# Writing out every engine's queue order in a fused decoder step, in place of pins, priorities and a chain

## The chip, the cores and the metric

The kernel runs on one core of a Trainium2 chip. The core has TensorE (PE in the profile, its weight loads PEld), VectorE (DVE), ScalarE (ACT), GpSimd (POOL) and SyncE (SP), each with a queue of its own that it works off in order; an instruction at the head of a queue waits by semaphores for what other engines and transfers have to deliver, and what stands behind it on that engine waits with it. The metric is device time in microseconds (us) of one execution, the median over runs.

## The reference

One layer of a decoder with two token mixers, run on a prompt of 512 tokens and on 8 sample tokens that have 1024 cached positions each; D_MODEL is 1024, heads are 64 wide.

```python
shift, scale, gate = jnp.split(jax.nn.silu(c) @ w_ada + b_ada, 3, axis=-1)
h = x * (1.0 + scale[:, None, :]) + shift[:, None, :]
parts = jnp.split(h @ w_in, np.cumsum(IN_WIDTHS)[:-1], axis=-1)
(a_q, a_kc, a_vc, a_ks, a_vs, a_kw, a_vw, a_g, a_z, b_q, b_k, b_v, b_z, m_a, m_b) = parts
...
ck = compress(cmp_seq[:, :, 0], phi_pos[0], phi_w1[0], phi_b1[0], phi_w2[0], phi_b2[0])   # gelu(blk @ w1 + b1) @ w2 + b2
cv = compress(cmp_seq[:, :, 1], phi_pos[1], phi_w1[1], phi_b1[1], phi_w2[1], phi_b2[1])
...
o_a = nsa_attention(...)     # gates[0] * compressed + gates[1] * selected blocks + gates[2] * window
o_b = moba_attention(...)    # top blocks by q . mean(k), and the own block
y_a = (o_a.reshape(bsz, t, NSA_WIDTH) * jax.nn.silu(a_z)) @ w_up_a
y_b = (o_b.reshape(bsz, t, MOBA_WIDTH) * jax.nn.silu(b_z)) @ w_up_b
mixed = (jax.nn.sigmoid(m_a) * y_a + jax.nn.sigmoid(m_b) * y_b) @ w_out
x_new = layer_norm(DEEPNORM_ALPHA * x + gate[:, None, :] * mixed, ln_g, ln_b)
```

The new rows of each cache are outputs as well.

## The kernel before

Everything runs in fp32 on TensorE's fp32r path, where each product is made of three matmuls: both operands are split into a high part (a cast, mostly on ACT: weights `hl` at L305, cache rows `u` at L877) and the rest (`lo`, a subtraction on DVE or POOL, L226). A dense product `d` thus takes `hTh` with both parts of the weights and `hTl` with the high part, all through `mm` (L172); transposes go through `tr` (L191).

The stages, by the time of the profile: the adaLN vectors and the modulated input (0 to 42 us); the compression network "phi" over the prompt and over four pairs of cache pages (42 to 145), in which a page is loaded into `craw`, split into `u`, multiplied with the first weight matrix (`s<-u,w1h`), put through a gelu (`t1`, then `gl`, split like the rest), and multiplied with the second (`pt<-gl,w2h`); the sample tokens' compressed branch (145 to 181); attention of eight head pairs for the prompt, with the sample tokens' decode over cache pages between them (181 to 507); the last of that decode (to 536); the up and output projections (536 to 626); the norms (to 647). Dense products ("fills", lists of column blocks of w_in and others) are interleaved with all stages but the last by `merge`, which takes the next step of the flow that is furthest behind its planned time.

Loads are issued by SP through `ld` (L199) and by POOL for gathers. The weights come through a feed of 4 raw buffers and 3 split ones, decode pages (`raw<-slck`, `raw<-mobk`, `raw<-mobv`) through a ring of their own, so a load's issue waits until its buffer was last read.

The order of each engine's queue is settled by a scheduler that simulates the program, bound by what the code pins. `order` adds a dependency without a semaphore, used for `in_turn` (while `behind[0]` is set, TensorE's instructions stay in the order of the trace) and for the chain of loads in `ld` (once `queue[0]` is set). `issue_after` keeps an instruction behind another one's issue, `high_priority` lifts it in the scheduler. `together` keeps the matmuls of a group adjacent, and can make the first of them wait, with a semaphore, for instructions given to it: in `value` these are three copies of transposed probabilities.

In the attention the scores `s` of a head come through `probs` (DVE adds the bias and takes the maximum at L1096, ACT exponentiates at L1099, DVE takes the reciprocal at L1100, POOL or DVE scales at L1101), are transposed to `pt`, copied to `pp` (L1110) and multiplied with the values to `o`.

## Time and profile before

| | |
|---|---|
| median of 3 runs | 648.98 us (646.98 to 650.88) |
| profiled execution, own time | 648.92 us |
| its span, first to last instruction | 647.1 us |
| mean granted TensorE clock | 0.976 |
| TensorE busy | 604.3 us (93%) |
| weight loads, DVE, ACT, POOL busy | 509.2, 320.7, 296.4, 289.5 us |
| DMA | 124.80 MB, mean 193 GB/s |

The busy times are added over the whole span, so they hide which stage waits for what; the waits and the stretches shown with the prediction tell that. A matmul's "mean ns" is its latency, and matmuls overlap, so the number of matmuls times that is more than the busy time. The granted clock is the share of full speed at which TensorE was allowed to run.

### The profile page before, as it was taken

To read this page: it belongs to the slowest core of one execution; us is meant where nothing else is said; L and a number is where in the kernel's file an instruction comes from. 1 tells how busy PE (TensorE), PEld (TensorE's weight loads), DVE (VectorE), ACT (ScalarE), POOL (GpSimd) and SP (SyncE) were. 2 spreads that over 40 slices of the span, in tenths; PEclk is the share of its full clock that TensorE was granted. 3 is DMA by queue.
4 is the path that set the end of the run, shared out by engine and by line. 5 is a ranking of instruction groups with operands and counts; after the bars stand their busy time and mean duration, and the time that the engine had idled before them with its cause. 6 is when DMAs were issued, how large, how long until landed. Compare 5 with 4: busy or idle time off the path is not lost.

```text
span 647.1 us, 13273 instructions
## 1 busy us (share of the span) xinstructions
PE 604.3 (93%) x4709; PEld 509.2 (79%) x4709; DVE 320.7 (50%) x818; ACT 296.4 (46%) x680; POOL 289.5 (45%) x328
## 2 busy tenths in 40 slices
PE   5999899979999999999998999989999989999993
PEld 2789799979988868867767898977766669799672
DVE  3467365342476558545454454684432125545277
ACT  3367355423446537645444455555442232433621
POOL 2033665442463623532435634363332326465646
PEclk9999899969999999999999999999999989999997
DMA  8985645422345495268895754712878966344302
GB/s 313 406 286 185 195 148 158 144 73 66 98 128 168 146 332 192 75 224 273 277 349 172 236 185 156 226 49 71 276 264 304 403 231 214 132 165 141 120 31 102
DMA packets 63956, 124.80 MB, mean 193 GB/s; under 512 B 8402, under 2 KB 26642, under 8 KB 63378
## 3 DMA queue, kind: packets, MB, share of 16 engines
q1 hardware_dynamic: 62482, 119.76, 55.0%
q0 software_dynamic: 1408, 4.20, 1.9%
q8 instruction: 37, 0.61, 0.4%
q14 instruction: 29, 0.24, 0.1%
HBM read 114.34 MB, written 9.58 MB: 191 GB/s over the span
## 4 chain that ended last, share of the span: by engine, by line
PE 58%; DMA 7%; DVE 7%; issue 5%; SPq 4%; ACT 4%; POOL 2%; POOLq 0%; ACTq 0%; DVEq 0%
PE d L172 33%; PE s L172 8%; PE e L172 6%; SPq L199 4%; PE pt L191 3%; PE o L175 2%; PE o L172 2%; DMA craw<-cmp 2%; DMA raw<-w_cols 2%; DMA xw<-bw 1%; PE pt L172 1%; PE e L175 1%; DMA raw<-slcv,vidx 1%; DMA raw<-mobk 1%; DVE u L226 1%
## 5 line engine op out<-in xcount | busy, mean ns | idle before, releaser
L172 PE MATMUL d<-hTh,hl 128*128 128x260 f32 (+1 forms) x1408 | 273.7, 291 | 1.5 <-DVE hl L226 1.0
L172 PEld LDWEIGHTS d<-hTh,hl 128*128 128x128 f32 (+1 forms) x1408 | 218.7, 188 | 25.3 <-issue 18.5
L172 PE MATMUL d<-hTl,hl 128*128 128x260 f32 (+1 forms) x704 | 199.6, 283 | 0.0
L172 PEld LDWEIGHTS d<-hTl,hl 128*128 128x128 f32 (+1 forms) x704 | 131.9, 187 | 0.3
L226 POOL TENSOR_TENSOR hl<-raw,hl 128x512 fp32r<-128x512 f32 x57 | 74.9, 1314 | 89.0 <-ACT hl L305 85.6
L305 ACT CAST hl<-raw 128x512 fp32r<-128x512 f32 (+1 forms) x111 | 67.9, 616 | 73.1 <-PE d L172 62.2
L1099 ACT ACTIVATE p<-s,sm 128x512 f32<-128x512 f32 (+1 forms) x96 | 50.6, 528 | 69.5 <-DVE sm L1096 57.1
L1101 POOL TENSOR_SCALAR p<-p,sm,gp 128x512 f32<-128x512 f32 (+1 forms) x64 | 42.7, 669 | 75.1 <-DVE sm L1100 73.5
L226 DVE TENSOR_TENSOR hl<-raw,hl 128x512 fp32r<-128x512 f32 (+1 forms) x54 | 51.5, 953 | 48.0 <-ACT hl L305 47.3
L172 PE MATMUL d<-yh,hl 128*128 128x260 f32 x256 | 46.6, 284 | 0.0
L191 PE MATMUL pt<-cst,p 128*128 128x128 f32 x240 | 39.3, 279 | 2.5 <-POOL p L1101 1.8
L172 PEld LDWEIGHTS d<-yh,hl 128*128 128x128 f32 x256 | 39.6, 188 | 2.4 <-ACT yh L1485 0.8
L1096 DVE CUSTOM_DVE_ANT_0 s<-s,band 128x256 f32<-128x256 f32 (+1 forms) x48 | 17.4, 363 | 47.5 <-PE s L172 42.2
L1101 POOL TENSOR_SCALAR p<-p,sm,cst 128x512 f32<-128x512 f32 (+3 forms) x32 | 20.4, 640 | 39.7 <-DVE sm L1100 39.5
L172 PE MATMUL s<-u,w1h 128*128 128x256 f32 (+1 forms) x160 | 33.7, 307 | 3.1 <-POOL u L226 3.1
L172 PE MATMUL d<-yl,hl 128*128 128x260 f32 x128 | 35.8, 284 | 0.4 <-DVE yl L226 0.4
L172 PE MATMUL s<-kd,q 128*128 128x512 f32 (+1 forms) x96 | 33.3, 346 | 1.3 <-ACT p L1099 1.3
L191 PEld LDWEIGHTS pt<-cst,p 128*128 128x128 f32 x240 | 27.7, 142 | 7.6 <-POOL p L1101 4.7
L226 POOL TENSOR_TENSOR u<-craw,u 128x512 fp32r<-128x512 f32 x16 | 22.6, 1419 | 21.1 <-ACT u L877 20.1
L172 PEld LDWEIGHTS s<-u,w1h 128*128 128x128 f32 x160 | 28.7, 217 | 3.3 <-POOL u L226 3.3
L172 PE MATMUL s<-kd,qx 128*128 128x512 f32 (+1 forms) x96 | 30.9, 322 | 0.0
L172 PEld LDWEIGHTS s<-kd,q 128*128 128x128 f32 x96 | 18.2, 189 | 15.2 <-issue 8.3
(417 smaller groups left out, 1141.7 us busy)
## 6 DMA issues: line engine op xcount, KB each, us to landing
raw<-w_cols SPq DMA_DIRECT2D x46, 512.0 KB, 5.0
raw<-mobk SPq DMA_DIRECT2D x64, 256.0 KB, 4.1
raw<-mobv SPq DMA_DIRECT2D x64, 256.0 KB, 4.9
craw<-cmp SPq DMA_DIRECT2D x64, 128.0 KB, 2.2
u<-ada_ss SPq DMA_DIRECT2D x12, 512.0 KB, 9.0
raw<-slck SPq DMA_DIRECT2D x64, 64.0 KB, 2.1
raw<-ada_g SPq DMA_DIRECT2D x8, 512.0 KB, 4.7
raw<-w_up SPq DMA_DIRECT2D x8, 512.0 KB, 4.8
```

Source lines behind the costliest of these rows:

```text
L172: i = mmraw(out, lhsT, rhs, start=start, stop=stop, skip_group_check=True)
L175: i = mmraw(out, lhsT, rhs, start=start, stop=stop, skip_group_check=True)
L191: return in_turn(nc.tensor.transpose(out, x, unit))
L199: i = nc.sync.dma_start(out, x)
L226: (nc.gpsimd if eng == "p" else nc.vector).tensor_sub(out, x, f32(hi))
L305: nc.scalar.copy(h, src)
L1096: nc.vector.tensor_tensor_reduce(out=s[:, b:n], in0=s[:, b:n], in1=j.band[:, 256 - (n - b):], scale=1.0, scalar=top, op0=OP.add, op1=OP.mi ...
L1099: nc.scalar.activation(pr, s[:, :n], AF.Exp, scale=-1.0, bias=sm[:, 1:2], accum_out=sm[:, 2:3])
L1101: D.setdefault("pool", []).append(nc.gpsimd.tensor_scalar(pr, pr, sm[:, 3:4], j.gate(i), op0=OP.mult, op1=OP.mult))
```

## The change

A table `QUEUES` lists, for each of the five engines, runs of indices into that engine's instructions in the order in which the program makes them, and `line_up`, called once after the kernel is built, turns each list into a chain of dependencies without semaphores. What pinned the order before is taken out: `order`, `in_turn`, `together` (with its semaphore waits on the three copies), `issue_after` and `high_priority` at all their places, and the chain of loads. `behind` becomes `steady`, a mere flag, and `queue[0]` becomes `D['late']`, which still sets how far ahead weights are loaded.

```diff
+QUEUES = {
+    "PE": """
+0-471 521-526 473-496 472 497-520 527-886 932-937 896-919 887-895 920-931 938-1275 1288-1289 1276-1287 1290-1363 1368-1371 1364-1367 1372-1379
...
+}
...
+def line_up(tc):
+
+    traced = tc.nc.cur_bb.bb.instructions
+    for name, text in QUEUES.items():
+        mine = [i for i in traced if i.engine == getattr(mybir.EngineType, name) and i.opcode != "TilePoolBoundary"]
+        queue = []
+        for run in text.split():
+            a, _, b = run.partition("-")
+            queue += mine[int(a):int(b or a) + 1]
+        assert len(queue) == len(mine) == len({i.name for i in queue})
+        for before, i in zip(queue, queue[1:]):
+            tc.add_manual_dep(i, before.name, mybir.DependencyInfo(mybir.DependencyClass.NoSync, mybir.DependencyReason.DATA),
+                              reason="queue")
...
-    glue, behind, queue = [False, None], [False, None], [False, None]
+    steady = [False]
 
     def mm(out, lhsT, rhs, start, stop):
-        if glue[1] is None:
-            i = mmraw(out, lhsT, rhs, start=start, stop=stop, skip_group_check=True)
...
-        return in_turn(i)
+        return mmraw(out, lhsT, rhs, start=start, stop=stop, skip_group_check=True)
...
     def ld(out, x):
-
-        i = nc.sync.dma_start(out, x)
-        if queue[0]:
-            if queue[1] is not None:
-                order(i, queue[1])
-            queue[1] = i
-        return i
+        return nc.sync.dma_start(out, x)
...
-            with tc.high_priority():
-                return gelu(us, n)
+            return gelu(us, n)
...
-            with together([js[1].copied[k] for k in range(3)]):
-                for kb in range(4):
...
+            for kb in range(4):
```

Against the queues of before, 75 of TensorE's 4209 instructions move, 15 of 578 on ACT, 19 of 722 on DVE, 8 of 330 on POOL and 3 of 514 on SP; the others keep their order. Most moves stand at 0 to 13, 73 to 85, 129 to 145, 181 to 245, 327 to 390, 429 to 447, 478 to 509 and 519 to 530 us of the profile. Three of the places follow; in the changed kernel line numbers are higher (L172 becomes L244, L175 is its sibling form, L191 becomes L247, L226 becomes L260, L641 becomes L667).

POOL at 69 to 78 us, in the first compression stage: `u_794` is the small part of a cache page, `gd` the sample tokens' gates, which eight small transfers rearrange, `hl_994` and `hl_1130` weights of the dense fills. Before:

```order
L226 TENSOR_TENSOR u_795<-craw_842,u_795 128x4x16x8
L641 DMA gd_82<-gs_922 8x1x3 x8
L226 TENSOR_TENSOR hl_994<-raw_819,hl_994 128x512
L226 TENSOR_TENSOR u_794<-craw_885,u_794 128x4x16x8
L226 TENSOR_TENSOR hl_1130<-raw_819,hl_1130 128x512
L226 TENSOR_TENSOR u_1091<-craw_958,u_1091 128x4x16x8
```

Now:

```order
L260 TENSOR_TENSOR u_795<-craw_842,u_795 128x4x16x8
L667 DMA gd_82<-gs_922 8x1x3 x2
L260 TENSOR_TENSOR u_794<-craw_885,u_794 128x4x16x8
L667 DMA gd_82<-gs_922 8x1x3 x2
L260 TENSOR_TENSOR hl_994<-raw_819,hl_994 128x512
L667 DMA gd_82<-gs_922 8x1x3 x4
L260 TENSOR_TENSOR hl_1130<-raw_819,hl_1130 128x512
L260 TENSOR_TENSOR u_1091<-craw_958,u_1091 128x4x16x8
```

The second split of `u_794` (from `craw_885`) stands behind two of the eight transfers in place of all eight and a weight split.

TensorE at 129 us, at the end of the compression stage: `pt_1778` is the second product of a page pair's network, which reads the gelu `gl_1616`; `s_1791` is the first product of the next pair's; `d_1831` and `d_1699` are dense fills. Before:

```order
L172 MATMUL d_1699<-hTl_74,hl_1702 128x260
L172 MATMUL pt_1778<-gl_1616,w2h_113 128x256
L172 MATMUL pt_1778<-gl_1616,w2l_114 128x256
L172 MATMUL pt_1778<-gl_1616,w2h_113 128x256
L172 MATMUL pt_1778<-w2h_113,gl_1616 128x64
L172 MATMUL pt_1778<-w2l_114,gl_1616 128x64
L172 MATMUL pt_1778<-w2h_113,gl_1616 128x64 x2
L172 MATMUL pt_1778<-w2l_114,gl_1616 128x64
L172 MATMUL pt_1778<-w2h_113,gl_1616 128x64
L172 MATMUL s_1791<-u_1619,w1h_111 128x256
L172 MATMUL s_1791<-u_1619,w1l_112 128x256
L172 MATMUL s_1791<-u_1619,w1h_111 128x256 x2
```

Now:

```order
L244 MATMUL d_1699<-hTl_74,hl_1702 128x260
L244 MATMUL d_1831<-hTh_73,hl_1751 128x260 x2
L244 MATMUL d_1831<-hTl_74,hl_1751 128x260
L244 MATMUL d_1831<-hTh_73,hl_1751 128x260 x2
L244 MATMUL d_1831<-hTl_74,hl_1751 128x260
L244 MATMUL s_1791<-u_1619,w1h_111 128x256
L244 MATMUL s_1791<-u_1619,w1l_112 128x256
```

Six dense matmuls of `d_1831` and all 24 of `s_1791` stand ahead of `pt_1778`, which follows behind the last of `s_1791`. On POOL the split of `gl_1616` goes ahead of one of `u_1620` at the same place.

TensorE at 520 us: `e_6597` is the product of the last mobv cache page with the sample tokens' probabilities `tp_5955`; `d_7080` is an up projection, `d_6962` and `d_6963` are dense fills. Before:

```order
L172 MATMUL d_7080<-yh0_6744,hl_6966 128x260 x2
L172 MATMUL d_7080<-yl0_6745,hl_6966 128x260
L172 MATMUL e_6597<-raw_6903,tp_5955 32x512
L175 MATMUL e_6597<-raw_6903,tp_5955 32x512 x3
L172 MATMUL d_6963<-hTh_73,hl_6884 128x260 x2
L172 MATMUL d_6963<-hTl_74,hl_6884 128x260
```

Now:

```order
L244 MATMUL d_6962<-hTh_73,hl_6929 128x260 x2
L244 MATMUL d_6962<-hTl_74,hl_6929 128x260
L244 MATMUL e_6597<-raw_6903,tp_5955 32x512 x4
L244 MATMUL d_6963<-hTh_73,hl_6929 128x260 x2
L244 MATMUL d_6963<-hTl_74,hl_6929 128x260
```

`e_6597` stands behind 18 dense matmuls (the second half of a block of `d_6963` and twelve of `d_6962`) that it preceded.

Around 431 us, on ACT the exponential of a score block (`p_5871`) goes ahead of an evacuation, a weight cast and a copy to `pp`; on DVE a weight split (`hl_5911`) goes behind two reciprocals and the scaling `xm`; on TensorE the four transposes `pt_5942` go 18 matmuls later.

## The prediction

> **What bounds the kernel now.** I read the page first, for the busy shares and the clock row, then the view of what the engines wait for, cut to TensorE, then a table of stretches around the longest of those waits, and last the timeline at four places.

> ```profile
> span 647.1 us, 13273 instructions
> PE 604.3 (93%) x4709; PEld 509.2 (79%) x4709; DVE 320.7 (50%) x818; ACT 296.4 (46%) x680; POOL 289.5 (45%) x328
> ```

> TensorE is busy 604.3 of 647.1 us; no other engine passes half. So the time is TensorE's work, its idle time, and the time in which it works at half clock. The second is this list (engine, line, what it waited for: us in total, times, longest):

> ```profile
> PE s L172 <- DMA u<-ada_ss: 7.5, 4, 5.1
> PE s L172 <- POOL u L226: 3.1, 1, 3.1
> PE e L172 <- DMA raw<-mobv: 3.0, 1, 3.0
> PE pt L172 <- ACT gl L817: 2.9, 1, 2.9
> PE pt L191 <- ACT pp L1110: 1.9, 4, 0.8
> PE e L172 <- DMA raw<-slcv,vidx: 1.9, 1, 1.9
> PE pt L191 <- POOL p L1101: 1.8, 1, 1.8
> PE pt L172 <- POOL gl L226: 1.5, 1, 1.5
> PE s L172 <- ACT p L1099: 1.3, 2, 1.1
> PE pt L172 <- DVE gl L226: 1.1, 1, 1.1
> PE d L172 <- DVE hl L226: 1.0, 1, 1.0
> PE d L191 <- DVE v L607: 0.8, 1, 0.8
> PE d L191 <- ACT ev L576: 0.6, 1, 0.6
> PE d L172 <- ACT hl L305: 0.5, 1, 0.5
> ```

> These rows sum to 28.9 us, and seven shorter ones of the view, none above 0.5, add some 2: waits of single instructions at the head of TensorE's queue, behind which everything else on it stands. The half clock is in the stretches (start:end, length, then busy time of PE, its weight loads, DVE, ACT and POOL, the granted clock, DMA share, GB/s):

> ```profile
> 76.60:80.20 3.60, 3.59 (x18) 3.59 (x19) 0.00 (x0) 0.00 (x0) 1.19 (x1) 0.55 0.67 172
> 129.27:134.44 5.17, 0.80 (x2) 0.50 (x2) 4.43 (x5) 3.33 (x8) 5.09 (x5) 0.73 0.68 205
> 134.44:141.00 6.56, 6.55 (x30) 6.56 (x31) 2.11 (x5) 0.72 (x2) 1.18 (x1) 0.50 0.06 21
> 353.30:356.60 3.30, 3.28 (x64) 3.12 (x64) 0.00 (x0) 0.00 (x0) 0.00 (x0) 0.53 0.02 5
> 436.00:438.40 2.40, 2.40 (x12) 2.40 (x12) 1.02 (x4) 0.79 (x3) 1.15 (x2) 0.50 0.01 3
> 523.40:527.20 3.80, 3.75 (x19) 2.67 (x20) 0.69 (x1) 0.62 (x1) 0.11 (x1) 0.60 0.13 50
> 536.00:626.00 90.00, 90.00 (x570) 75.57 (x569) 42.20 (x77) 34.24 (x54) 52.47 (x53) 1.00 0.41 138
> ```

> Behind the waits of 3.1, 2.9 with 1.5, 1.9, 1.1 with 1.8, and 3.0 us the clock falls to about 0.5 for some 3.4 us; in 90 us without a wait it stays at 1.00. A half-speed piece of 3.4 us does 1.7 us of work, so it costs 1.7 us, and a wait of 3 us costs 4.8. The 1.5 us at 507 (1.0 for hl on DVE, 0.5 on ACT) were followed by a stretch at 1.00, quoted below. So the trigger lies between 1.5 and 1.9 us of idle in one piece. At full clock the chain of work that ended last has one row for 54 matmuls in a line, 0.12 us each:

> ```profile
> 145.23 6.46 PE d L172 x54
> ```

> [...]

> **The change part by part.** It adds and removes no instruction, tile or copy, so the busy time at full clock is unchanged. The waits that `together` set on three copies cost nothing before: no row of that view is an `o` matmul. What is left is the place of the moved instructions; 75 of TensorE's 4209 move, and a few on each of the others.

> S1, 73 us. The matmuls s_1025 need the small part u_794, on POOL:

> ```profile
> 69.67 4.39 POOL L641 DMA_DIRECT2D gd<-gs  x8
> 74.07 1.27 POOL L226 TENSOR_TENSOR hl<-raw,hl 128x512 fp32r<-128x512 f32 x1
> 75.30 1.26 POOL L226 TENSOR_TENSOR u<-craw,u 128x512 fp32r<-128x512 f32 x1
> 83.92 0.36 ACT L804 COPY bsh<-s 64x256 f32<-64x256 f32 x1 [1.46 <-PE s L172]
> 82.01 1.29 POOL L226 TENSOR_TENSOR u<-craw,u 128x512 fp32r<-128x512 f32 x1 [4.22 <-ACT u L877]
> 84.96 1.12 DVE L226 TENSOR_TENSOR u<-craw,u 128x512 fp32r<-128x512 f32 x1 [0.15 <-ACT u L877]
> ```

> Eight DMA issues (4.39/8 = 0.55 each) and a split of 1.27 stood ahead of it. Now only two issues do: 69.67 + 1.1 + the split's 1.26, held a little by its ACT half, ends near 72.5, a microsecond before TensorE reaches it at 73.5; six d_940 matmuls (0.7) now stand ahead as well. The 3.09 and the half-speed piece (1.7) go: 4.8 at TensorE. But the next cache page is loaded and split behind the last s_1050 (ACT at 83.92, DVE to 86.08), and it moves by 3.1 + 1.7 less the six matmuls that now run first: 4.1 to 4.2. I take 4.2, range 3.1 (the wait alone) to 4.8. The six remaining issues and the hl split come later on POOL; POOL idles 4.22 us before its next u split at 82.01, which covers them.

> S2, 129 to 145 us.

> ```profile
> 131.98 1.73 POOL L226 TENSOR_TENSOR u<-craw,u 128x512 fp32r<-128x512 f32 x1
> 133.66 0.73 POOL L226 TENSOR_TENSOR gl<-t,gl 128x256 fp32r<-128x256 f32 x1
> 130.68 1.14 ACT L877 CAST u<-craw 128x512 fp32r<-128x512 f32 x2 [0.59 <-DMA craw<-cmp]
> 131.33 1.25 DVE L226 TENSOR_TENSOR u<-craw,u 128x512 fp32r<-128x512 f32 x1 [0.43 <-ACT u L877]
> ```

> At 129.27 six d_1831 matmuls now stand first (0.73 at full clock, to 130.0). s_1791 is next; its last u piece is cast on ACT by 131.25 and split on DVE by 132.6, both bound by the load that lands at 130.68. The 22 matmuls left take 2.8, to 135.4; pt_1778 (0.9) then finds its gl split, which now stands ahead of the 1.73 us u split on POOL; s_1816 (2.9, and 0.1 for its end) is done at 139.3. The row of 54 matmuls has that end at 145.23: 5.9 us. But 1.3 + 1.0 us of idle are left between 130.0 and 132.6, and 2.3 is above the 1.9 that sufficed at 351, so I charge one half-speed piece: 5.9 - 1.7 = 4.2. Low end 1.7 (three half-speed pieces remain, the waits shrink), high end 5.9.

> S6, 431 us. TensorE waits 1.1 (a score buffer, freed by an exp on ACT) and 1.8 (p on POOL).

> ```profile
> 432.44 0.69 ACT L1099 ACTIVATE p<-s,sm 128x512 f32<-128x512 f32 x1
> 431.96 2.56 DVE L226 TENSOR_TENSOR hl<-raw,hl 128x512 fp32r<-128x512 f32 x1
> ```

> The exp of p_5871 now stands ahead of the evacuation, the weight cast and the pp copy on ACT (0.37 + 0.61 + 0.37), which gives the 1.08; the DVE split of 2.56 us, behind which the reciprocals waited, now stands behind them; and the four transposes pt_5942 stand behind 18 matmuls more (d, e, s, d: 2.2 us). All of 2.9 and the half-speed piece (1.7, of which the stretch from 436 to 438.4 shows 1.2) should go, and xn for 446, one of the short waits (under 0.5), moves up. Together some 4.8; I take 4.3 for one short wait left, range 2.0 (the piece and a wait stay) to 4.8. The 2.56 us split feeds d_6056, which stands over 50 matmuls (6 us) further on: that covers its move.

> S8, 520 us. The last mobv page (3.00 us of wait) is issued here:

> ```profile
> 513.12 2.75 SPq L199 DMA_DIRECT2D raw<-mobv  x4
> ```

> The four e_6597 matmuls now stand behind 18 d matmuls whose weights are there (18 x 0.12 = 2.2). 3.00 - 2.2 leaves 0.8, below the trigger, so the half-speed piece (1.7) goes too: 2.2 + 1.7 = 3.9, less 0.1 for the reordering: 3.8. Low 2.1 (the piece stays), high 4.7 (all goes).

> Small ones. S3, 181 to 213 us: the v copy goes ahead of a split on DVE (v 0.8), and two short waits get cover: 0.9, from 0 to 1.3. S4, 213 to 245: e behind 18 d matmuls (a wait on slck under 0.5) and the load of xw three issues earlier, behind which DVE held up the pp copies (0.8 of their 1.9): 1.0, from 0 to 1.1. S5, 327 to 390: a transpose 16 matmuls later (ev 0.6) and scores behind six d (a wait of 0.2): 0.8, from 0.4 to 0.8. S0, the start: SP now issues the first ada half ahead of the cT table; one issue is at most 0.7 by the row at 513 (2.75/4), and the first wait of 5.1 ends with the second half's landing, so 0.2, from -0.7 to 0.7. S7, 478 to 509: a weight cast now stands ahead of two others on ACT, though its load lands late; 0.2, from -0.7 to 0.7, half of the 1.5 there either way.

> The waits for gl on DVE (1.1), slcv (1.9, with its half-speed piece), one pp copy (0.7) and the last 111 us are not touched.

> Sum: 0.2 + 4.2 + 4.2 + 0.9 + 1.0 + 0.8 + 4.3 + 0.2 + 3.8 = 19.6. The profiled execution took 648.92 us (1.82 outside its span), 0.06 below the median 648.98, so nothing is corrected: 648.9 - 19.6 = 629.3. The low ends sum to 7.9 (-0.7 + 3.1 + 1.7 + 0 + 0 + 0.4 + 2.0 - 0.7 + 2.1), which gives 641.0; the high ends to 24.8 (0.7 + 4.8 + 5.9 + 1.3 + 1.1 + 0.8 + 4.8 + 0.7 + 4.7), which gives 624.1.

> **The rivals.**

> A, 629.3: as worked out, the freed time is carried to the end because the loads follow the buffers that TensorE frees.

> B, short waits still trip the clock at S6 and S8 as well: 1.9 us was enough at 351, and shorter waits in one piece add up. Two pieces more are 3.4: 632.7. For it: the trigger's place rests on two rows.

> F, what is left at S2 doesn't trip it: 1.3 and 1.0 us are parted by two matmuls and may fall into two pieces. Then S2 gives 5.9 and the time is 627.6. Against it: 353, where 1.9 sufficed. [...]

> C, the loads set the pace between 446 and 520 and hold the last mobv page where it is:

> ```profile
> 446.00:480.00 34.00, 33.58 (x254) 23.76 (x254) 14.04 (x51) 15.06 (x41) 12.71 (x17) 1.00 0.80 257
> 480.00:507.00 27.00, 26.77 (x206) 17.56 (x204) 5.63 (x9) 6.77 (x17) 5.82 (x6) 1.00 0.86 306
> 507.00:520.00 13.00, 11.50 (x93) 9.30 (x90) 2.73 (x3) 3.82 (x8) 5.64 (x5) 1.00 1.03 398
> ```

> The queues are nearly full, and 15.6 us of the sum lie ahead of them. If the landing at 523.4 stays, only S8's 3.8 remains: 645.1. Against it: the idle share (0.20 x 34 + 0.14 x 27 = 10.6 us) need not even be used, since transfers that start earlier end earlier. Half of it, a late page that takes back 8, gives 637.

> D, slower: the clock answers to load, not to idleness. Where the moves pack TensorE closest (60 to 145, 431 to 536) half-speed pieces would come at 1.7 each; from (19.6 + 3.2)/1.7 = 14 of them on the kernel is slower by over 0.5%, at 652.2 or more. Against it stands the row of 90 us at 1.00 with TensorE never idle.

> E, the order does little, since each new head of TensorE's queue meets its own late input. That nothing moves is excluded, by the order itself. If every wait comes back at half its price, the sum is 9.8 and the time 639.1. For it: at S2 I see such a remainder myself. Against it: at S1 and S8 what now stands first is ready by 1 us and more.

> **How the numbers follow.** A 0.42, B 0.14, F 0.10, C 0.16 (most of it at the half), E 0.12, D 0.06. The predicted time is A's, 629.3. A, B and F reach from 624 to 633; C's half and E lie at 637 and 639, so the range is 623 to 639.5. 0.5% is 3.2 us, about what a measurement of this kernel can tell from no change. Faster by more: A, B, F (0.66) and most of C and E (0.24), 0.90; within: the rest of C and E and a little of D, 0.05; slower: the rest of D, 0.05.

> **What would show it.** In the profile after, TensorE's rows of 3.1 (POOL u), 3.0 (mobv), 2.9 (ACT gl), 1.8 (POOL p) and 1.5 (POOL gl) should be gone or under 1.4, with a mean granted clock near 0.985 or above; slcv's 1.9 should remain. The mobv wait should be near 0.8; if it is 3 or more, C holds. A wait of s on u of 2 to 2.5 at about 125 to 128 is S2's remainder. What would make me wrong: the same idle in fresh places, such as pt on p or d on hl in the attention, where splits were put behind others.

## The result, and the profile after

The changed kernel takes 626.84 us (median of 4 runs, 624.57 to 628.10) against 647.98 us (4 runs, 646.02 to 650.88): a ratio of 0.9666, 95% interval 0.9617 to 0.9715, 21.1 us less by the medians. The forecast was 629.3 us in a range from 623 to 639.5. The profiled execution of the changed kernel is its fastest, 624.57 us, so its trace shows 24.3 us less than the trace of before; the two must not be mixed.

The head of the page after:

```profile
span 622.8 us, 13266 instructions
PE 595.3 (96%) x4709; PEld 502.5 (81%) x4709; DVE 319.7 (51%) x818; ACT 295.8 (47%) x680; POOL 288.5 (46%) x328
```

Of the 24.3 us of span, TensorE's idle time gives 15.3 (647.1 - 604.3 = 42.8 before, 622.8 - 595.3 = 27.5 after) and its busy time 9.0. It does the same 4709 instructions, so the 9.0 is half-speed work that is now done at full clock (ahead of the norms TensorE was busy at a clock of 0.50 for 21.4 us in the trace of before and for 3.4 in this one, and half of the difference is 9.0): the mean granted clock rose from 0.976 to 0.990. What TensorE waits for, after:

```profile
PE s L244 <- DVE cs L537: 5.5, 1, 5.5
PE s L244 <- DMA u<-ada_ss: 2.0, 2, 1.8
PE e L244 <- DMA raw<-slcv,vidx: 1.4, 1, 1.4
PE pt L244 <- DVE gl L260: 1.3, 2, 1.1
PE d L244 <- ACT hl L338: 1.0, 1, 1.0
PE s L244 <- ACT u L890: 0.7, 1, 0.7
PE pt L247 <- ACT pp L1117: 0.7, 1, 0.7
PE s L244 <- DVE u L260: 0.7, 2, 0.5
PE s L244 <- ACT a L470: 0.5, 1, 0.5
PE s L244 <- DMA raw<-ada_g: 0.5, 1, 0.5
```

The rows of 3.1 (POOL u), 3.0 (mobv), 2.9 (ACT gl), 1.8 (POOL p), 1.5 (POOL gl) and 1.1 (ACT p) are gone; nothing above 1.4 us is left after the start. The stretches that answer to those of before (same columns):

```profile
76.60:80.20 3.60, 3.60 (x32) 3.58 (x31) 1.88 (x3) 1.51 (x3) 3.59 (x5) 1.00 0.21 60
127.70:134.00 6.30, 6.08 (x49) 5.87 (x50) 5.20 (x8) 3.49 (x9) 4.99 (x5) 1.00 0.33 107
340.20:344.00 3.80, 3.80 (x78) 3.52 (x79) 0.98 (x3) 0.02 (x1) 1.31 (x3) 1.00 0.27 34
418.00:422.00 4.00, 4.00 (x37) 4.00 (x36) 2.36 (x12) 2.77 (x10) 3.73 (x5) 1.00 0.03 6
484.20:488.10 3.90, 2.05 (x14) 0.74 (x13) 1.03 (x2) 1.68 (x4) 0.19 (x1) 1.00 1.01 386
488.10:491.50 3.40, 3.40 (x19) 2.17 (x18) 0.00 (x0) 0.74 (x2) 3.40 (x4) 0.50 1.03 383
512.00:602.00 90.00, 90.00 (x570) 75.53 (x568) 42.18 (x77) 34.23 (x54) 52.62 (x53) 1.00 0.40 137
```

All places that ran at half speed before run at 1.00, the one behind slcv too, which the change does not touch. One new half-speed stretch stands at 488, where TensorE was idle for 1.85 us of the 3.9 before it (three waits, 0.5 on ada_g and 1.0 and 0.3 on a late weight). The 90 us at the end are as they were.

### The profile page after: what moved, and what is told of

It is laid out like the page before. It is cut to its first block, busy times and chain, and to the rows that moved or that the text cites. A ratio compares the mean times of both kernels' runs of the same rounds, so it can differ in the third digit from the quotient of the medians.

```text
span 622.8 us, 13266 instructions
## 1 busy us (share of the span) xinstructions
PE 595.3 (96%) x4709; PEld 502.5 (81%) x4709; DVE 319.7 (51%) x818; ACT 295.8 (47%) x680; POOL 288.5 (46%) x328
## 4 chain that ended last, share of the span: by engine, by line
PE 77%; DMA 8%; DVE 6%; SPq 3%; issue 2%; POOL 2%; ACT 2%; POOLq 0%; ACTq 0%; DVEq 0%
PE d L244 45%; PE s L244 11%; PE e L244 8%; PE o L244 6%; PE pt L247 4%; SPq L250 2%; DMA raw<-w_cols 2%; PE pt L244 2%; DMA craw<-cmp 2%; DMA u<-ada_ss 1%; DMA raw<-wink 1%; DMA raw<-mobk 1%; DMA raw<-slcv,vidx 1%; POOL u L260 1%; DVE u L260 1%
## 5 line engine op out<-in xcount | busy, mean ns | idle before, releaser
L244 PE MATMUL d<-hTh,hl 128*128 128x260 f32 (+1 forms) x1408 | 272.4, 290 | 1.4 <-ACT hl L338 1.0
L244 PEld LDWEIGHTS d<-hTh,hl 128*128 128x128 f32 (+1 forms) x1408 | 218.0, 187 | 23.6 <-issue 17.1
L244 PE MATMUL d<-hTl,hl 128*128 128x260 f32 (+1 forms) x704 | 199.4, 283 | 0.0
L244 PEld LDWEIGHTS d<-hTl,hl 128*128 128x128 f32 (+1 forms) x704 | 131.6, 187 | 0.3
L260 POOL TENSOR_TENSOR hl<-raw,hl 128x512 fp32r<-128x512 f32 x57 | 74.2, 1302 | 82.8 <-ACT hl L338 65.7
L260 DVE TENSOR_TENSOR hl<-raw,hl 128x512 fp32r<-128x512 f32 (+1 forms) x54 | 46.4, 859 | 45.6 <-ACT hl L338 45.1
L244 PE MATMUL d<-yh,hl 128*128 128x260 f32 x256 | 46.6, 284 | 0.0
L244 PEld LDWEIGHTS d<-yh,hl 128*128 128x128 f32 x256 | 39.7, 188 | 2.4 <-ACT yh L1482 0.8
L247 PE MATMUL pt<-cst,p 128*128 128x128 f32 x240 | 38.6, 275 | 0.1
L244 PE MATMUL d<-yl,hl 128*128 128x260 f32 x128 | 35.8, 284 | 0.4 <-DVE yl L260 0.4
L244 PE MATMUL s<-kd,q 128*128 128x512 f32 (+1 forms) x96 | 33.9, 353 | 0.1
L244 PE MATMUL s<-u,w1h 128*128 128x256 f32 (+1 forms) x160 | 30.1, 285 | 1.5 <-ACT u L890 0.7
L247 PEld LDWEIGHTS pt<-cst,p 128*128 128x128 f32 x240 | 27.6, 141 | 4.2 <-POOL p L1109 1.9
L244 PE MATMUL s<-kd,qx 128*128 128x512 f32 (+1 forms) x96 | 31.0, 322 | 0.0
L1108 DVE RECIPROCAL sm<-sm 128x1 f32<-128x1 f32 x96 | 15.4, 160 | 29.8 <-ACT p L1107 29.4
L244 PEld LDWEIGHTS s<-kd,q 128*128 128x128 f32 x96 | 18.1, 188 | 14.8 <-issue 8.9
L1117 ACT COPY pp<-pt 128x512 f32<-128x512 f32 (+1 forms) x48 | 23.0, 478 | 13.7 <-PE pt L247 13.2
```

What stands on the lines that cost most here:

```text
L244: return mmraw(out, lhsT, rhs, start=start, stop=stop, skip_group_check=True)
L247: return nc.tensor.transpose(out, x, unit)
L260: (nc.gpsimd if eng == "p" else nc.vector).tensor_sub(out, x, f32(hi))
L1108: D["chain"] = nc.vector.reciprocal(sm[:, 3:4], sm[:, 2:3])
L1117: j.copied[gi] = (nc.scalar.copy if COPY_ENG[gi] == "a" else nc.vector.tensor_copy)(t[:, :n], p[:, :n])
```

## The experiments

The order table makes it possible to put back the moves of one place alone: each kernel below is the changed program with some runs of the table written as before. A place's step is how much the end of the same matmul, unmoved by the change, comes earlier against the trace of before, behind the place less ahead of it. It comes from one profiled execution each, and leaves out the time won or lost at the other places. The trace of before is one execution too: e1, which has the same order, differs from it by 1.9 us at S2 and by -1.4 at S6, so a step is no surer than that. Times are medians, and ratios stand against the kernel before on the same chip; the runs stand on several chips, on which the kernel before had medians from 646.52 to 648.42 us, so a difference of medians between two of them is the rougher number.

**e1, the order of before in the table.**

```diff
 "PE":
-0-471 521-526 473-496 472 497-520 527-886 932-937 896-919 887-895 920-931 938-1275
+0-1275
...
```

(and so on, at every place and on every engine)

> The changed program with a table that holds the order of before on every engine: only the pins, the priorities and the waits of the three copies are gone. Theory A (the gain is all in the moved instructions): 648 us, from 646 to 651, the same waits of TensorE as before (3.1 on POOL u, 2.9 and 1.5 on gl, 1.8 on p, 3.0 on mobv) and a granted clock near 0.976. Rival B (taking away pins and semaphore waits pays by itself): below 644 us, with shorter waits in the attention.

648.96 us (10 runs, 644.15 to 651.34), ratio 1.0013 (0.9980 to 1.0047). Its waits:

```profile
PE pt L244 <- ACT gl L832: 2.4, 1, 2.4
PE s L244 <- POOL u L260: 2.3, 1, 2.3
PE e L244 <- DMA raw<-slcv,vidx: 1.9, 1, 1.9
...
PE pt L247 <- POOL p L1109: 1.8, 1, 1.8
...
PE e L244 <- DMA raw<-mobv: 1.1, 3, 0.4
```

Theory A holds: taking away the pins, the priorities and the semaphore waits changes the time by no more than the interval, -0.2% to 0.5%, so the gain is in the moves. The wait on POOL u is 2.3 where 3.1 was expected. The mobv row shows something more: 1.1 us in place of 3.0 with the same order. In this execution the loads' lag met TensorE earlier, at 505 to 511 (0.4, 0.6, 0.9 and 1.3 us of idle).

**e2, all but S1.**

```diff
 "PE":
-521-526 473-496 472 497-520
+472-526
 "Pool":
-31 27 26 32 25 28-30
+25-30 32 31
```

(and three groups of ACT and two of DVE at that place)

> The changed kernel with the order of before for the moves of S1 (67 to 93 us). Theory A (what S1 gives is carried on, less the 1.4 us that comes back at 95 and 111): 630.3 us, 3.5 more than the changed kernel's 626.8, with the wait of 3.1 on POOL u and its half-speed piece back. Rival C (the loads of the compression stage set the pace to 134 us, so S1's gain comes back there): 628 us or less.

630.73 us, ratio 0.9761 (0.9701 to 0.9821): 3.9 above the changed kernel by the medians, as A had it, though the two intervals overlap by 0.0014. TensorE's wait is back, and the stretch behind it ran at half clock:

```profile
PE s L244 <- POOL u L260: 4.1, 2, 3.5
```

With S1's moves the step was 4.9 us in each of the nine profiles that have them; 0.3 to 1.4 of it come back between 88 and 128 us, as waits for the next pages' splits. The rest is carried on: e2's trace is 5.3 us behind the changed kernel's at 500 us, and 3.6 at the end, since it lost less at the late weights, which the next runs are about.

**e3, all but S7; e6, all but S7 and S8; e11, all but S8.**

```diff
 "PE" (S7, S8):
-3254-3255 3248-3253 ... 3314-3319 3294-3313 ... 3512-3529 3508-3511
+3248-3255 ... 3294-3319 ... 3508-3529
 "Activation" (S7):
-498 495-496
+495-496 498
```

(the first two PE pieces and the row of ACT are S7, with one pair more on ACT and one on DVE; the last PE piece is S8)

> The changed kernel with the order of before for the moves of S7 (477 to 509 us). In the changed kernel TensorE waits 0.5, 1.0 and 0.3 us there and then has a half-speed piece, 2.0 us in all. Theory A (the weight cast put ahead of two others on ACT makes it): the piece goes, 624.8 us, 2 less than the changed kernel's median. Rival C (the queues are full there, and the weights land late whatever the order): 626 to 628 us, TensorE still waits 1.5 us or more in all at that place.

> The changed kernel with the order of before from 460 us on (S7 and S8). Theory A (S8 covers the wait for the last mobv page and gives what was forecast): 630 us or more, 3 to 5 above the changed kernel's 626.8, with the mobv wait of 3 us or the same time in waits for weights at 485 to 490. Rival C (the loads are behind in this stretch by an amount that differs from one execution to another, and the order moves only the place of the wait): 626.5 to 628.5.

> The changed kernel with the order of before for S8 alone (the last mobv product ahead of the 18 d matmuls again). With S7 and S8 both as before it took 629.1 us, with S7 alone as before 628.1, as changed 626.8 and 627.1. Theory A (S8 by itself covers the last page's wait, worth 2 to 4 us): 629 to 630 us, with a wait on mobv of 2 to 3 us and a half-speed piece behind it. Rival C (the lag of the loads shows at 485 to 490 instead, and S8 gives little): 627 to 628 us, with less than 1.5 us of wait on mobv.

e3: 628.10 us, ratio 0.9699 (0.9642 to 0.9755). Theory A falls: with the cast back in its old place the wait is there all the same, and longer:

```profile
PE d L244 <- ACT hl L338: 2.5, 1, 2.5
```

e6: 629.13, 0.9726 (0.9686 to 0.9766), between the two expectations. e11: 629.82, 0.9726 (0.9660 to 0.9792), as A had it. In both, the last mobv page is waited for, and a half-speed stretch follows (the row of waits of e6, that of e11, and e11's stretch behind the longest):

```profile
PE e L244 <- DMA raw<-mobv: 2.8, 1, 2.8
...
PE e L244 <- DMA raw<-mobv: 4.0, 3, 3.2
...
504.40:507.80 3.40, 3.40 (x16) 1.86 (x9) 0.69 (x1) 0.15 (x1) 0.00 (x0) 0.50 0.18 69
```

So S8 is worth 2 to 3 us by the medians against the changed kernel, and 1.0 by e6 against e3, where S7 is missing from both. The intervals of all four kernels overlap, so the times alone don't settle it; the traces do show that the wait is back. S7 and S8 together stepped by 2.6 to 4.2 and once (e8) by 1.0 us in the seven profiles that have both, and by 0.1 (e6), 0.4 (e3) and -0.4 (e11) where one or both are missing. What the order didn't set is how late the weight at 485 to 490 lands: TensorE's idle there was 0.3 (e2) to 3.4 us (e8) over the profiles of the changed kernel and of its variants, at a DMA share of about 1.0. Over all thirteen traces this same 512 KB load landed 6.3 to 9.5 us after its issue, 6.7 in e2 and 9.5 in e8. Whether S7 by itself gives anything is not settled; e3's interval holds the changed kernel's ratio.

**e4, S2 alone on the order of before.**

```diff
 "PE" (against e1):
-887-937
+932-937 896-919 887-895 920-931
 "Activation":
-140 133
+133 140
 "DVE":
-126 131
+131 126
 "Pool":
-63 58
+58 63
```

> The order of before with the moves of S2 alone (129 to 145 us). The changed kernel gained 6.9 us there where 4.2 was forecast. Theory A (the moves do it by themselves: TensorE's remaining wait is 1 us and no half-speed piece comes): the step at 145 us is 6.9 us, and one execution takes about 642 us. Rival (it needed S1's earlier split and shift; alone it leaves 2.3 us of wait and a half-speed piece): the step is 4.2 us, about 645 us.

One execution took 643.24 us; the step at S2 is 7.2. Of the waits for gl on ACT (2.9) and POOL (1.5) none is left, and the next on u is short:

```profile
PE s L244 <- ACT u L890: 0.4, 1, 0.4
```

Theory A holds in this one execution: the moves do it by themselves, with neither S1 nor anything else. How much they give depends on the trace that they are held against. Before ran at half clock for 10.2 us from 131.6 on, e1, with the same order, for 6.8; against e1 the steps at S2 are 1.9 smaller, 5.4 here and 5.1 in the changed kernel.

**e5, all but S0** (the pairs on SP, ACT and DVE of the first 45 us back, on SP `1 0` becomes `0-1`).

> The changed kernel with the order of before for the moves of S0 (the first 45 us: SP's first two loads, two pairs on ACT, three on DVE). The kernels with the new start waited 5.4 to 5.6 us at first, those with the old one 5.1. Theory A (the new start costs rather than gives): first wait 5.1, 626.2 us, about 0.6 less than the changed kernel's 626.8. Rival (the start's waits differ by chance from one execution to another): 626.8, and a first wait of 5.4 or more.

624.83 us, but ratio 0.9665 (0.9617 to 0.9713), which is the changed kernel's. By the profile the first wait is 5.3 us, and the first 55 us end 0.1 earlier than before, where they end 0.5 later in the first profile of the change; the six others with the new start range from 0.2 earlier to 2.9 later. The new start seems to cost about half a microsecond; the times don't show it.

**e8, all but S6** (PE `2989-3010`, `3011-3024`, `3034-3041` in line again, and the rows of ACT, DVE and POOL there).

> The changed kernel with the order of before for the moves of S6 (429 to 447 us). Theory A (S6's gain stands by itself: waits of 1.1 and 1.8 us and the half-speed piece behind them): these waits are back, with a granted clock of 0.5 over 3.4 us behind them, and one execution takes about 631.5 us. Rival (the loads hold back what S6 gains): the waits are back, but the time is under 629.

One execution, 634.01 us. The waits and the half-speed stretch behind them are back as they were:

```profile
PE pt L247 <- POOL p L1109: 1.8, 1, 1.8
...
PE s L244 <- ACT p L1107: 1.1, 1, 1.1
```

```profile
422.50:426.00 3.50, 3.50 (x19) 3.50 (x18) 1.25 (x4) 1.98 (x6) 2.18 (x3) 0.51 0.03 7
```

The step at S6 is -0.2; with the moves it is 4.2 to 4.5 in every profile. That the time is 2.5 over the expectation comes from other places: 3.4 us of waits and a half-speed stretch at 493 to 500, and one behind slcv.

**e7, more moves; e10, one more; e9, the changed kernel beside it.** e7 has the old start and four moves of my own on what was left in the list of waits; e10 adds six dense matmuls ahead of s_1791.

```diff
 "PE":
-2285-2294 ... 2369-2414
+2289-2294 2285-2288 ... 2403-2414 2369-2402
 "Activation":
-116 98
+98 116
 "DVE":
-122 114 121
+114 121-122
 e10, "PE":
-896-919 887-895 920-931 938-955
+950-955 896-919 887-895 920-931 938-949
```

> The changed kernel with the old start (S0), and four more moves: twelve d matmuls ahead of the slcv product (its wait was 1.4 to 2.0 us, sometimes with a half-speed piece of 1.7), six d ahead of the transposes of c (wait 0.7), and at 108 us the gelu's split and one u split ahead of a weight split on DVE, the gelu's cast ahead of a weight cast on ACT (0.5 of 1.6). Theory A (a wait at the head of TensorE's queue costs its length wherever it stands): 0.6 + 1.4 + 0.7 + 0.5 and half a piece, some 3.5 us: 623.3 us. Rival (the loads that TensorE then meets earlier take it back): 626 to 627.

> The changed kernel once more, on the same chip as the next one, so that the two can be compared. Every theory: 625 to 628 us; the same waits as before, with the waits at 127 (u on ACT), 340 (slcv) and 485 to 488 (weights) differing by up to a microsecond or two, since they hang on when a transfer lands.

> The kernel with the old start and four more moves, and in it six more d_1831 matmuls ahead of s_1791 at 127 us, where TensorE still waited 0.8 to 1.6 us for a page's cast. Theory A (waits at the head of the queue add up, and a wait under 1.5 us costs its length): 3.5 to 4 us under the changed kernel on the same chip. Rival (the compression stage and the decode are paced by their loads, which come no earlier): 1.5 us or less under it.

e7: 623.75 us, ratio 0.9651 (0.9619 to 0.9682). The time is near A's 623.3, but on that chip the kernel before is faster as well (646.54 us where it was 647.98), and the ratio is not told apart from the changed kernel's; e5, the old start without the four moves, is 1.1 us above e7 on the same chip. So e7 by itself doesn't settle A. e9: 627.13, 0.9660 (0.9620 to 0.9701). e10: 622.45, 0.9599 (0.9559 to 0.9639): 4.7 us under the changed kernel on the same chip, a little more than A's 3.5 to 4; the two intervals still overlap by 0.002, but e10's slowest run (624.86) is about e9's fastest (624.31). The slcv wait is 0.3 where it was 1.4 to 2.0:

```profile
PE e L244 <- DMA raw<-slcv,vidx: 0.3, 1, 0.3
```

So part of what was left could be had in the same way. e10 has the lowest median of all kernels run here.

## Why the prediction was right, and which terms were off

The mechanism was as told: the waits of 3.1, 2.9 with 1.5, 1.9, 1.1 with 1.8, and 3.0 us at the head of TensorE's queue are gone but for 1.4 at slcv and 1.0 at S2, the 3.41 us (10.24 at S2) at a clock of 0.50 behind each of them too, and the loads came earlier as TensorE did: the last four of mobv were issued from 492.50 us on, where it was 513.12 before. That the total came so near is in part luck: terms that were too low and too high cancel, and the profile's 24.1 is 4.5 above the forecast's sum where the medians' 21.1 is 1.5 above. The terms, against the steps of the profiles (the first of the changed kernel; then the range over all profiles that have the moves in the table of the change):

| place | forecast | first profile | range |
|---|---|---|---|
| S0, start | 0.2 | -0.5 | -2.9 to 0.2 |
| S1, less what comes back to 128 us | 4.2 | 3.6 | 3.4 to 4.5 |
| S2 | 4.2 | 6.9 | 4.7 to 7.2 |
| S3 | 0.9 | 1.5 | 1.3 to 1.9 |
| S4 | 1.0 | 1.0 | 0.0 to 1.4 |
| S5 | 0.8 | 1.2 | 1.2 |
| slcv, 350 to 358 (not moved) | 0 | 2.1 | 0.1 to 2.1 |
| S6 | 4.3 | 4.4 | 4.2 to 4.5 |
| 446 to 495 | in S6 and S7 | 1.1 | 0.3 to 1.1 |
| S7 and S8 | 4.0 | 2.6 | 1.0 to 4.2 |
| sum, with 0.2 at other places | 19.6 | 24.1 | |

S1 came as worked out (a step of 4.9 where 4.8 was forecast, and 0.3 to 1.4 given back where 0.6 was); on POOL the second split of u_794 now ends at 73.7 where TensorE asks at 74.5:

```profile
71.01 1.33 POOL L667 DMA_DIRECT2D gd<-gs  x2
72.36 1.30 POOL L260 TENSOR_TENSOR u<-craw,u 128x512 fp32r<-128x512 f32 x1
```

S2 is the step that was mis-sized. I had the last split of u on DVE last 1.25 us, as before, and so 2.3 us of idle and a half-speed piece. After, the cast, the split and TensorE's two waits read:

```profile
126.96 0.62 ACT L890 CAST u<-craw 128x512 fp32r<-128x512 f32 x1 [1.48 <-DMA craw<-cmp]
127.61 0.69 DVE L260 TENSOR_TENSOR u<-craw,u 128x512 fp32r<-128x512 f32 x1 [2.25 <-ACT u L890]
128.18 1.29 POOL L260 TENSOR_TENSOR hl<-raw,hl 128x512 fp32r<-128x512 f32 x1 [1.64 <-ACT hl L338]
127.63 0.39 PE L244 MATMUL s<-u,w1h 128*128 128x256 f32 x1 [0.75 <-ACT u L890]
128.36 0.51 PE L244 MATMUL s<-u,w1h 128*128 128x256 f32 x2 [0.22 <-DVE u L260]
```

The split takes 0.69, with POOL idle beside it until 128.18, where before POOL split all through DVE's 1.25 (more below), and the page lands closer to the time at which TensorE asks. Idle was 1.0 us, and no half-speed piece came. Held against e1 in place of the trace of before, S2 gives 5.1, so what it is worth is known to no better than some 2 us. In the other profiles the wait on u was 0.4 to 1.6, and only in e6 did a piece follow; there the step is 4.7, near the forecast's 4.2.

slcv was not foreseen. I took its piece as fixed, but a wait of 1.4 to 2.0 us was followed by a half-speed piece or not: of the eight profiles that have the changed order around it, four had no half-speed piece and a step of 1.7 to 2.1, four had one and a step of 0.1 to 0.2. Half of 2.1 on the average is missing from the sum. The trigger as I told it, between 1.5 and 1.9 us of idle in one piece, is wrong: e5's 1.68 us at slcv was followed by a piece and the 1.8 of e6 and of e11 were not, and at 488 three waits of 1.03 at most were. What the traces show of it is told below.

S8 was forecast too high together with S7, since the lag of the loads, put down by rival C to the mobv page, shows up at 485 to 490 as well. That part of C held, at some 1 to 3 us; the stronger part, that the loads give back what was gained ahead of them, did not: S6 and all before it is carried on in every kernel, but for the few microseconds by which the idle at the late weight differs. Pieces behind short waits came now and then (at slcv, at 488), as B said, but not at S6 or S8. F's outcome is the one that came, no piece at S2, and 626.84 is nearer to its 627.6 than to A's 629.3; its reason, that 2.3 us fall into two pieces, was not put to the test, since only 1.0 was idle. D's outcome did not come: the granted clock rose from 0.976 to 0.990 while TensorE's busy share rose from 93% to 96%, though three pieces in the other traces came behind no idle at all (below). E is out, except for S2's remainder.

## What to carry to other kernels

Rank the waits of the busiest engine by length, and look for work behind each that does not need what is waited for: with such work left where it stood (e1) the ratio to the kernel before was 1.0013, with it moved ahead 0.9666. Over the thirteen traces, all eleven of TensorE's single waits of 2.3 us or more after the start were followed by a half-speed piece, and so were twelve of the twenty between 1.5 and 2.2: as an estimate from that for this kernel, count the first as their length plus 1.7 us (3.41 us at a clock of 0.50), the second as either, and one of about 1 us as its length (behind the 1.1 on gl, at 112.24 us before and at 108.56 after, the clock stayed at 1.00), but add up several within one stretch of 3.4 us (0.5, 1.0 and 0.3 us ahead of 488 were followed by a piece). At the late weight, with a DMA share of about 1.0, the idle was 0.3 us in e2 and 3.4 in e8, which have the same order there, so cost such a place from more than one execution.

## What the runs showed of the hardware

```profile
345.11 0.64 PE L244 MATMUL e<-raw,tp 128*32 128x128 f32 x16 [1.71 <-DMA raw<-slcv,vidx]
...
345.20:349.00 3.80, 3.80 (x79) 3.52 (x79) 0.98 (x3) 0.05 (x1) 1.31 (x2) 1.00 0.34 39
```

```profile
338.85 0.74 PE L244 MATMUL e<-raw,tp 128*32 128x128 f32 x12 [1.68 <-DMA raw<-slcv,vidx]
...
339.00:342.50 3.50, 3.50 (x65) 3.12 (x59) 0.00 (x0) 0.00 (x0) 0.00 (x0) 0.51 0.02 5
```

Behind the longer wait the clock stayed at 1.00, behind the shorter one it was 0.51. Within one profile all half-speed pieces start on one grid of 3.41 us: in e1 they start at 61.46, 78.52, 133.14, 351.59, 433.51, 512.02 and 532.50, each 5, 16, 64, 24, 23 and 6 times 3.413 us behind the one ahead of it; in the trace of before they start at 76.99, 131.60, 353.47, 435.39 and 524.14, 16, 65, 24 and 26 times that apart, behind stretches that were idle for 0.89, 0.68, 0.56, 0.61 and 0.80 of their length. In e2 a mark at 343.7 cuts the wait, and 0.40 of the stretch behind it is idle; in e5 the whole wait falls into one stretch, 0.49 of it. Laid over the idle time of the thirteen profiles, each full-speed stretch of the grid after the start that was idle for 0.50 or more of its length was followed by a piece (but for one of 0.54 in the norms at the end of e1), between 0.43 and 0.49 four were and five not, and none of 0.42 or less was, but for three that were not idle at all: before 61.5 and 532 in e1, and 511 in e9. What set those off stays open. So of two waits of 1.7 us one was followed by 3.4 us at half clock, which cost 1.7 us more, and the other was not, and they differ in how they lie to the marks.

**In the changed kernel's trace a split of 128x512 on DVE took 0.69 us with POOL mostly idle and 1.33 beside a TENSOR_TENSOR of POOL (medians); POOL's own median did not move.** The splits of weights (minimum, median and maximum in ns):

```profile
L260 POOL TENSOR_TENSOR hl<-raw,hl x57: 1259/1286/1737, 42.5 to 574.3; 128x512 fp32r<-128x512 f32 x57
L260 DVE TENSOR_TENSOR hl<-raw,hl x54: 346/692/1840, 43.9 to 575.5; 128x512 fp32r<-128x512 f32 x53, 128x192 fp32r<-128x192 f32 x1
```

Of the 69 DVE splits of 128x512 for weights and pages, the 34 during which POOL was busy for less than half of the time have a median of 0.69 us, and the seven beside other work of POOL have 0.69 too; the 28 during half or more of which POOL ran a TENSOR_TENSOR have a median of 1.33 and range from 0.68 to 2.03, a factor of about two on the median and of three at most. POOL's own median is 1.29 whether DVE is busy beside it or not. By DVE's split at S2, 1.25 us before and 0.69 now, this made, as an estimate, some half a microsecond of what S2 gave over its forecast.
